# GpSimd's wide elementwise work is given to VectorE in a two-layer hybrid encoder, and the norm's steps are put in a new order

## The chip, the cores and the metric

The kernel runs on one core of one Trainium2 chip. The metric is the device time of one execution in microseconds (us), and a kernel's time is the median over its runs. TensorE (PE in the profile) multiplies matrices, VectorE (DVE) and ScalarE (ACT) do elementwise work and reductions, GpSimd (POOL) is a programmable engine that can do elementwise work too, and SyncE (SP) issues the transfers of the weights.

## The reference

256 tokens of width 1024 pass through two layers. Each layer has a SwiGLU FFN, a token mixing with three groups of heads, and a second FFN; every one of these six sub-layers is wrapped in an RMSNorm before and an RMSNorm after. Cut to what matters here:

```
for l in range(2):
    f = swiglu(rmsnorm(x, ffn1_pre_g[l]), ...);  x = x + 0.5 * rmsnorm(f, ffn1_post_g[l])
    m = token_mixing(rmsnorm(x, mix_pre_g[l]), ...);  x = x + rmsnorm(m, mix_post_g[l])
    f = swiglu(rmsnorm(x, ffn2_pre_g[l]), ...);  x = x + 0.5 * rmsnorm(f, ffn2_post_g[l])

# token mixing: one projection, three groups of heads, one output projection
A: softmax(q k^T / 8 + bias[head, clipped distance]) v            # 6 heads, bias is learned
B: (softmax(s0 + alibi) - lam * softmax(s1 + alibi)) v, normed      # 4 heads, alibi = -slope * distance
C: z = q k^T / 8;  a = exp(log_sigmoid(z) + suffix sum of log_sigmoid(-z)) v   # 6 heads, strictly causal
```

## The kernel before

All weights stream from memory in chunks of 512 KB. Each chunk is cut into a high and a low part: ScalarE rounds the chunk (L142, tile `whi`), VectorE subtracts the rounded part from the chunk (L143, tile `wlo`). TensorE then makes three products for each block of weights (L379 to L381, or L411 and L413 in the FFN), so that the sum is nearly float32. A class `Stream` hands the chunks out in a fixed order, up to nine chunks ahead of TensorE (more late in a sub-layer, where free tiles are lent to it), and each call of `ahead` issues half-chunk cuts on ScalarE and VectorE at the place in the program where it is called.

Everything runs in the order in which it is written: each engine takes its own instructions in program order and waits only for the semaphores of the tiles that it needs.

In the token mixing (`mix`), the projections of the queries and keys are 16 column blocks `pp` (L379 to L381), each in four quarters. After each quarter `slot(n)` runs the events whose time in the table PLAN lies below n + 1: the steps of the heads of B (`head_b`), of the pairs of heads of C (`pair_c`), of the heads of A (`head_a`), the moving of a finished block into `qkT` on ScalarE (`evacuate`, L845 and L847), and cuts of weight chunks. So the attention of one layer is interleaved with its own projections.

A pair of heads of C goes through these steps: the scores on TensorE (`s_c`, L670 and L671); the mask and a copy on VectorE (`z_c`, L674 and L676); three passes on ScalarE (L678 to L680) and one on VectorE (L682), which leave -log_sigmoid(-z) in `e`; the cut of `e` into high parts on ScalarE (`h1`, `h0`, L688 and L689) and low parts on GpSimd (`l1`, `l0`, L690 and L691); the suffix sums on TensorE (`u_c`, L694 to L701); the subtraction on VectorE (L703 and L704); the exponential on ScalarE (L706); the product with the values on TensorE (`o_c`, L745 and L746). For pair 0 these steps have the times 27.1 to 44.15 in PLAN: the suffix sums at 39.1, the subtraction at 39.15, the exponential at 39.2, the product at 42.05. The bias of A is negated in one instruction (`make_bias`, L643, 128 partitions by 1536 elements) at 41.05. `make_alibi` scales the distances for the four heads of B (L593, four instructions) before the first projection block.

At the end of a sub-layer, `down` accumulates the output of both halves of the tokens (t = 0 and 1), and `Norm` then does three things for each half: the norm of the output (L317, L291, L286), the residual sum into `xs` (L329, two halves of the width), and the norm that the next sub-layer needs (`half_pre`, `end_pre`): the mean square on ScalarE (L299, tile `junk_pre`), its sum on VectorE (L291, `v_pre`), the power -1/2 on GpSimd (L286, `r_pre`), the product of `xs` with the weights of the norm (L359, the first half of the width on GpSimd, the second on VectorE), and the scaling (L365 on VectorE, L366 on ScalarE). TensorE then turns the result (L374, tile `pt`). There are five such places between the six sub-layers, with two halves of the tokens each. For t = 0 the work of TensorE on the last chunks of t = 1 covers the norm; for t = 1 the first blocks of the next sub-layer do. The covering is shorter after a token mixing, which has four chunks for it where an FFN has five.

Of the kernel before, what the change touches and what calls it, by code (L numbers as in the profile page):

```python
# [9 lines left out]
F32 = mybir.dt.float32  # L10
# [3 lines left out]
ALU = mybir.AluOpType  # L14
# [150 lines left out]
def trunk_kernel(  # L165
# [7 lines left out]
    nc = tc.nc  # L173
# [123 lines left out]
    def mean_square(src, ss, h, nm):  # L297
        junk = work.tile([P, 512], BF16, tag="junk", name=f"junk_{nm}_{h}", bufs=1)
        nc.scalar.activation(junk, src, AF.Square, scale=ROOT, accum_out=ss[:, h : h + 1])  # L299
# [5 lines left out]
    class Norm:  # L305
# [6 lines left out]
        def post(self, banks, weight, slack=lambda k: None, last=None):  # L312
            i, t, nm = self.i - 1, self.t, "post" + self.nm
            ss = small.tile([P, 4], F32, tag="ss", name=f"ss_{nm}")
            fg = work.tile([P, D], F32, tag="fg", name=f"fg_{nm}", bufs=1)
            def gained(h):
                nc.vector.scalar_tensor_tensor(fg[:, HALVES[h]], banks[h], weight, post_tiles[i][:, HALVES[h]],  # L317
                                               ALU.mult, ALU.mult)

            for h in range(2):  # L320
                mean_square(banks[h], ss, h, nm)
            gained(0)
            r = rstd_of(halves_mean(ss, nm), 1, nm)
            gained(1)
            slack(0)
            if last is None:
                self.begin_pre()
            for h in range(2):
                nc.vector.scalar_tensor_tensor(xs[:, t, HALVES[h]], fg[:, HALVES[h]], r[:, 0:1],  # L329
                                               xs[:, t, HALVES[h]], ALU.mult, ALU.add)  # L330
                if last is None:
                    self.half_pre(h)
                else:
                    last(t, h)
            if last is None:
                self.end_pre()
                slack(1)
# [14 lines left out]
            self.ss = small.tile([P, 4], F32, tag="ss", name=f"sp_{self.nm}")  # L352
            self.xg = work.tile([P, D], F32, tag="xg", name=f"xg_{self.nm}", bufs=1)

        def half_pre(self, h):
            t, sl = self.t, HALVES[h]
            mean_square(xs[:, t, sl], self.ss, h, "pre" + self.nm)
            eng = nc.gpsimd if h == 0 else nc.vector
            eng.tensor_mul(self.xg[:, sl], xs[:, t, sl], pre_tiles[self.i][:, sl])  # L359

        def end_pre(self):
            self.r = rstd_of(halves_mean(self.ss, "pre" + self.nm), 1, "pre" + self.nm)

            xg = self.xg
            nc.vector.tensor_scalar(xg[:, :512], xg[:, :512], self.r[:, 0:1], None, ALU.mult)  # L365
            nc.scalar.activation(xg[:, 512:], xg[:, 512:], AF.Copy, scale=self.r[:, 0:1])  # L366

# [213 lines left out]
    def mix(i, l, turn1):  # L581
# [6 lines left out]
        def make_alibi():  # L588

            nc.vector.scalar_tensor_tensor(dneg, dist, -1.0, dist, ALU.mult, ALU.max)  # L590
            for h in range(NH_B):
                slope = 2.0 ** (-8.0 * (h + 1) / NH_B)
                nc.gpsimd.tensor_scalar(out=alibi[:, h, :], in0=dneg, scalar1=slope, scalar2=None, op0=ALU.mult)  # L593
            nc.gpsimd.memset(alibi[0:64, :, 192:256], FAR)

        def make_lambda():
# [43 lines left out]
        make_alibi()  # L640

        def make_bias():
            nc.gpsimd.tensor_scalar(out=biasA, in0=biasA, scalar1=-1.0, scalar2=None, op0=ALU.mult)  # L643
            nc.gpsimd.memset(biasA[0:64, :, 192:256], FAR)


# [2 lines left out]
        def pair_c(j):  # L649
# [37 lines left out]
            h1, l1 = hl1[:, :256], hl1[:, 256:]  # L687
            nc.scalar.copy(h1, e[:, 512:])  # L688
            nc.scalar.copy(h0, e[:, :512])  # L689
            nc.gpsimd.tensor_sub(l1, e[:, 512:], h1.bitcast(F32))  # L690
            nc.gpsimd.tensor_sub(l0, e[:, :512], h0.bitcast(F32))  # L691
            yield
            u1 = psum.tile([P, 256], F32, tag="acc", name=f"u1_{nm}")
            nc.tensor.matmul(u1, lhsT=tri, rhs=h1, start=True, stop=False)  # L694
# [276 lines left out]
```

## Time and profile before

| | |
|---|---|
| median of 3 runs | 1038.41 us (1036.89 to 1039.23) |
| profiled execution, its own time | 1042.82 us |
| span of the profile | 1041.1 us |
| TensorE busy | 1018.3 us, 98% of the span |
| VectorE busy | 676.4 us, 65% |
| ScalarE busy | 588.8 us, 57% |
| GpSimd busy | 89.0 us, 9% |
| mean granted TensorE clock | 0.986 of full speed |

The span runs from the first to the last instruction of one profiled execution, and all times inside the profile count from its start. Busy means that at least one instruction of the engine is in work. A granted clock of 1.00 is TensorE's level of 2.4 GHz, 0.50 is its level of 1.2 GHz.

### The profile page before, as it was taken

Reading aid. Unit: us, or ns where it says so; the run is one execution under the profiler, and the core shown is the slowest. Engines: PE = TensorE matmul, PEld = TensorE weight load, DVE = VectorE, ACT = ScalarE, POOL = GpSimd, SP = SyncE. Lnnn points to the kernel's source line nnn. Section 1 sums busy time; section 2 is a strip of 40 time slices with the busy share of each in tenths; the row PEclk is TensorE's granted clock in tenths of the full one; section 3 lists DMA queues with packets and bytes.
Section 4 is the critical chain, followed back from the end, with each engine's and each line's share of the span. In section 5 each row is a group of like instructions: output and inputs, shape, how many; then the busy total and the mean of one; then the engine's idle time right before and its main releaser. Section 6 shows DMA issues by size and latency. Waiting matters only on the chain. (4 is left out here: it accounts for less than half of the span.)

```text
span 1041.1 us, 16033 instructions
## 1 busy us (share of the span) xinstructions
PE 1018.3 (98%) x5940; PEld 888.6 (85%) x5940; DVE 676.4 (65%) x1313; ACT 588.8 (57%) x1265; POOL 89.0 (9%) x105
## 2 busy tenths in 40 slices
PE   8899999999999999999999999999999999999997
PEld 7788888898887988888899888888998789888886
DVE  4576774668666677665566876656776665877642
ACT  5465654567655556654446666545666655756531
POOL 3100000111311100000030000002123020000000
PEclk9999999999899999999999999999998999999999
DMA  8866566566244366656726766664933334865631
GB/s 270 219 204 200 184 211 208 145 203 192 82 122 122 117 210 220 197 189 219 215 73 208 244 195 195 222 198 121 261 107 103 117 97 143 261 190 186 222 120 40
DMA packets 151005, 183.16 MB, mean 176 GB/s; under 512 B 5744, under 2 KB 134896, under 8 KB 150928
## 3 DMA queue, kind: packets, MB, share of 16 engines
q1 hardware_dynamic: 148448, 174.08, 54.2%
q0 software_dynamic: 2192, 7.54, 2.7%
q8 instruction: 46, 0.75, 0.3%
q10 hardware_dynamic: 288, 0.52, 0.1%
q14 instruction: 31, 0.25, 0.1%
HBM read 181.08 MB, written 1.05 MB: 175 GB/s over the span
## 5 line engine op out<-in xcount | busy, mean ns | idle before, releaser
L143 DVE TENSOR_TENSOR wlo<-raw,whi 128x512 fp32r<-128x512 f32 (+1 forms) x625 | 403.2, 700 | 169.2 <-ACT whi L142 168.7
L142 ACT CAST whi<-raw 128x512 fp32r<-128x512 f32 x630 | 350.0, 617 | 120.5 <-PE acc L381 70.8
L411 PE MATMUL pg<-xT,whi 128*128 128x512 f32 x576 | 205.5, 398 | 0.0
L411 PE MATMUL pu<-xT,whi 128*128 128x512 f32 x576 | 203.2, 395 | 0.0
L413 PE MATMUL pg<-xT,wlo 128*128 128x256 f32 x576 | 162.2, 282 | 0.0
L413 PE MATMUL pu<-xT,wlo 128*128 128x256 f32 x576 | 161.5, 280 | 0.0
L379 PE MATMUL acc<-whi,hh 128*128 128x512 f32 x352 | 137.2, 390 | 0.0
L381 PE MATMUL acc<-whi,hl 128*128 128x512 f32 x352 | 137.0, 389 | 0.0
L380 PE MATMUL acc<-wlo,hh 128*128 128x512 f32 x352 | 137.0, 389 | 0.0
L411 PEld LDWEIGHTS pg<-xT,whi 128*128 128x128 f32 x576 | 108.7, 189 | 25.2
L411 PEld LDWEIGHTS pu<-xT,whi 128*128 128x128 f32 x576 | 108.0, 187 | 25.3
L413 PEld LDWEIGHTS pg<-xT,wlo 128*128 128x128 f32 x576 | 109.7, 190 | 0.0
L413 PEld LDWEIGHTS pu<-xT,wlo 128*128 128x128 f32 x576 | 108.8, 189 | 0.0
L379 PE MATMUL pp<-xT,whi 128*128 128x256 f32 x256 | 78.9, 308 | 0.0
L379 PEld LDWEIGHTS acc<-whi,hh 128*128 128x128 f32 x352 | 66.1, 188 | 13.7
L381 PEld LDWEIGHTS acc<-whi,hl 128*128 128x128 f32 x352 | 66.1, 188 | 13.7
L380 PEld LDWEIGHTS acc<-wlo,hh 128*128 128x128 f32 x352 | 66.1, 188 | 13.5
L380 PE MATMUL pp<-xT,whi 128*128 128x256 f32 x256 | 74.4, 291 | 0.0
L381 PE MATMUL pp<-xT,wlo 128*128 128x256 f32 x256 | 74.2, 290 | 0.0
L286 POOL TENSOR_TENSOR r_post<-v_post,mhalf 128x1 f32<-128x1 f32 x12 | 6.6, 552 | 779.5 <-DVE v_post L291 779.5
L379 PEld LDWEIGHTS pp<-xT,whi 128*128 128x128 f32 x256 | 51.0, 199 | 7.7 <-issue 7.2
L418 ACT COPY side_pu<-pu 128x256 f32<-128x256 f32 x72 | 26.1, 368 | 47.9 <-PE pu L413 47.9
(247 smaller groups left out, 1559.0 us busy)
## 6 DMA issues: line engine op xcount, KB each, us to landing
raw<-in_ffn_w_gate_dram SPq DMA_DIRECT2D x88, 512.0 KB, 4.8
raw<-in_ffn_w_up_dram SPq DMA_DIRECT2D x88, 512.0 KB, 4.7
raw<-in_ffn_w_down_dram SPq DMA_DIRECT2D x88, 512.0 KB, 4.4
raw<-in_w_in_dram SPq DMA_DIRECT2D x36, 512.0 KB, 5.6
raw<-in_w_out_dram SPq DMA_DIRECT2D x16, 512.0 KB, 3.5
raw<-in_w_in_dram SPq DMA_DIRECT2D x8, 576.0 KB, 4.5
gpost<-in_ffn_post_g_dram POOLq DMA_DIRECT2D x4, 512.0 KB, 4.6
raw<-in_w_in_dram SPq DMA_DIRECT2D x4, 384.0 KB, 3.5
```

Source lines behind the costliest of these rows:

```text
L142: self.nc.scalar.copy(self.hi[:, a:b], raw[:, a:b])
L143: (lo or self.nc.vector).tensor_sub(self.lo[:, a:b], raw[:, a:b], self.hi.bitcast(F32)[:, a:b])
L286: nc.gpsimd.tensor_tensor(r[:, :width], v, mhalf[:, :width], ALU.pow)
L379: nc.tensor.matmul(ps, lhsT=ah, rhs=bh, start=first, stop=False)
L380: nc.tensor.matmul(ps, lhsT=ah, rhs=bl, start=False, stop=False)
L381: nc.tensor.matmul(ps, lhsT=al, rhs=bh, start=False, stop=last)
L411: nc.tensor.matmul(ps.rearrange("p a t -> p (a t)"), lhsT=wh[:, k % 4, cs], rhs=xT[:, k].rearrange("p a t c -> p (a t c)"), start=k == 0, ...
L413: nc.tensor.matmul(ps[:, 1, :], lhsT=wl[:, k % 4, cs], rhs=xT[:, k, 0].rearrange("p t c -> p (t c)"), start=False, stop=k == KT - 1)
L418: nc.scalar.copy(side, ps[:, 1, :])
```

## The change

Four pieces of elementwise work go from GpSimd to VectorE: the negated bias of A, the four scalings of ALiBi, the low parts of `e` in group C (two instructions for each of the three pairs of a layer), and the first half of the product with the norm's weights. The two products of the norm, one for each half of the width, now stand on VectorE after both residual sums; the first stands ahead of the sum of the mean squares, the second behind it. The mean squares are issued where they were. GpSimd keeps the powers, the memsets, the iota, its transfers and the few cuts of weight chunks at the start.

```diff
@@ Norm.post
-                    self.half_pre(h)
+                    mean_square(xs[:, t, HALVES[h]], self.ss, h, "pre" + self.nm)
@@ Norm
-        def half_pre(self, h):
-            t, sl = self.t, HALVES[h]
-            mean_square(xs[:, t, sl], self.ss, h, "pre" + self.nm)
-            eng = nc.gpsimd if h == 0 else nc.vector
-            eng.tensor_mul(self.xg[:, sl], xs[:, t, sl], pre_tiles[self.i][:, sl])
-
         def end_pre(self):
-            self.r = rstd_of(halves_mean(self.ss, "pre" + self.nm), 1, "pre" + self.nm)
-
-            xg = self.xg
+            t, xg, g = self.t, self.xg, pre_tiles[self.i]
+
+            nc.vector.tensor_mul(xg[:, :512], xs[:, t, :512], g[:, :512])
+            v = halves_mean(self.ss, "pre" + self.nm)
+            nc.vector.tensor_mul(xg[:, 512:], xs[:, t, 512:], g[:, 512:])
+            self.r = rstd_of(v, 1, "pre" + self.nm)
             nc.vector.tensor_scalar(xg[:, :512], xg[:, :512], self.r[:, 0:1], None, ALU.mult)
             nc.scalar.activation(xg[:, 512:], xg[:, 512:], AF.Copy, scale=self.r[:, 0:1])
@@ make_alibi
-                nc.gpsimd.tensor_scalar(out=alibi[:, h, :], in0=dneg, scalar1=slope, scalar2=None, op0=ALU.mult)
+                nc.vector.tensor_scalar(out=alibi[:, h, :], in0=dneg, scalar1=slope, scalar2=None, op0=ALU.mult)
@@ make_bias
-            nc.gpsimd.tensor_scalar(out=biasA, in0=biasA, scalar1=-1.0, scalar2=None, op0=ALU.mult)
+            nc.vector.tensor_scalar(out=biasA, in0=biasA, scalar1=-1.0, scalar2=None, op0=ALU.mult)
@@ pair_c
-            nc.gpsimd.tensor_sub(l1, e[:, 512:], h1.bitcast(F32))
-            nc.gpsimd.tensor_sub(l0, e[:, :512], h0.bitcast(F32))
+            nc.vector.tensor_sub(l1, e[:, 512:], h1.bitcast(F32))
+            nc.vector.tensor_sub(l0, e[:, :512], h0.bitcast(F32))
```

The lines behind the edit in `Norm` move up by three, so L643 becomes L640, L690 becomes L687, L703 becomes L700 and so on. Three places on VectorE in the first layer's mixing; the second layer has the same three. The first is the stretch from the cuts behind the last pass of pair 0 to the subtraction of its sums (`yb` holds the `e` of pair 0, `wlo` are low parts of weights, `o_b` are outputs of B). Before:

```order
L143 TENSOR_TENSOR wlo_2804<-raw_2576,whi_2803 128x512 x2
L785 TENSOR_SCALAR yb_2378<-o_b_1_2834,rib_1_2563 128x64 x2
L785 TENSOR_SCALAR yb_2378<-o_b_0_2782,rib_0_2556 128x64 x2
L143 TENSOR_TENSOR wlo_2856<-raw_2611,whi_2855 128x512 x2
L703 TENSOR_TENSOR z_c_0_2741<-z_c_0_2741,u_c_0_2889 128x256
L704 TENSOR_TENSOR z_c_0_2741<-z_c_0_2741,u_c_0_2892 128x512
```

With the change:

```order
L143 TENSOR_TENSOR wlo_2804<-raw_2576,whi_2803 128x512
L687 TENSOR_TENSOR hl_c_0_2818<-yb_2378,hl_c_0_2818 128x256
L688 TENSOR_TENSOR l_c_0_2817<-yb_2378,h_c_0_2816 128x512
L143 TENSOR_TENSOR wlo_2804<-raw_2576,whi_2803 128x512
L782 TENSOR_SCALAR yb_2378<-o_b_1_2834,rib_1_2563 128x64 x2
L782 TENSOR_SCALAR yb_2378<-o_b_0_2782,rib_0_2556 128x64 x2
L143 TENSOR_TENSOR wlo_2856<-raw_2611,whi_2855 128x512 x2
L700 TENSOR_TENSOR z_c_0_2741<-z_c_0_2741,u_c_0_2889 128x256
L701 TENSOR_TENSOR z_c_0_2741<-z_c_0_2741,u_c_0_2892 128x512
```

The two low parts of pair 0 (`hl_c_0`, `l_c_0`) now stand on VectorE, between two cuts of weights and ahead of the subtraction.

The second place follows at once: the masks of pair 1, its pass L682 and the cut behind it. Before:

```order
L674 TENSOR_TENSOR z_c_1_2900<-s_c_1_0_2902,negmask 128x2x128
L676 COPY z_c_1_2900<-s_c_1_0_2902 128x128
L674 TENSOR_TENSOR z_c_1_2900<-s_c_1_1_2907,negmask 128x2x128
L676 COPY z_c_1_2900<-s_c_1_1_2907 128x128
L143 TENSOR_TENSOR wlo_2913<-raw_2670,whi_2912 128x512
L682 SCALAR_TENSOR_TENSOR e_c_1_2901<-z_c_1_2900,e_c_1_2901 128x768
L143 TENSOR_TENSOR wlo_2913<-raw_2670,whi_2912 128x512
```

With the change:

```order
L671 TENSOR_TENSOR z_c_1_2900<-s_c_1_0_2902,negmask 128x2x128
L673 COPY z_c_1_2900<-s_c_1_0_2902 128x128
L671 TENSOR_TENSOR z_c_1_2900<-s_c_1_1_2907,negmask 128x2x128
L673 COPY z_c_1_2900<-s_c_1_1_2907 128x128
L143 TENSOR_TENSOR wlo_2913<-raw_2670,whi_2912 128x512
L679 SCALAR_TENSOR_TENSOR e_c_1_2901<-z_c_1_2900,e_c_1_2901 128x768
L640 TENSOR_SCALAR yb_2378<-yb_2378 128x1536
L143 TENSOR_TENSOR wlo_2913<-raw_2670,whi_2912 128x512
```

The bias (128x1536, in another part of the tile `yb`) stands behind the subtraction of pair 0 and behind the last VectorE pass of pair 1. On GpSimd it stood right behind the low parts of pair 0.

The third place is further down, from the rounding of pair 0's output (`yC`) to the subtraction of pair 1's sums. Before:

```order
L303 TENSOR_TENSOR yC_2985<-o_c_0_2945,yC_2985 128x256
L143 TENSOR_TENSOR wlo_2969<-raw_2753,whi_2968 128x512
L682 SCALAR_TENSOR_TENSOR yb_2378<-z_c_2_2950,yb_2378 128x768
L143 TENSOR_TENSOR wlo_3023<-raw_2825,whi_3022 128x512 x2
L703 TENSOR_TENSOR z_c_1_2900<-z_c_1_2900,u_c_1_3050 128x256
L704 TENSOR_TENSOR z_c_1_2900<-z_c_1_2900,u_c_1_3053 128x512
```

With the change:

```order
L303 TENSOR_TENSOR yC_2985<-o_c_0_2945,yC_2985 128x256
L687 TENSOR_TENSOR hl_c_1_2990<-e_c_1_2901,hl_c_1_2990 128x256
L688 TENSOR_TENSOR l_c_1_2989<-e_c_1_2901,h_c_1_2988 128x512
L143 TENSOR_TENSOR wlo_2969<-raw_2753,whi_2968 128x512
L679 SCALAR_TENSOR_TENSOR yb_2378<-z_c_2_2950,yb_2378 128x768
L143 TENSOR_TENSOR wlo_3023<-raw_2825,whi_3022 128x512 x2
L687 TENSOR_TENSOR hl_c_2_3039<-yb_2378,hl_c_2_3039 128x256
L688 TENSOR_TENSOR l_c_2_3038<-yb_2378,h_c_2_3037 128x512
L700 TENSOR_TENSOR z_c_1_2900<-z_c_1_2900,u_c_1_3050 128x256
L701 TENSOR_TENSOR z_c_1_2900<-z_c_1_2900,u_c_1_3053 128x512
```

Pair 1's low parts stand ahead of a cut and of pair 2's pass, and pair 2's low parts, which wait for ScalarE's rounding of pair 2, now stand ahead of pair 1's subtraction.

## Rows read from the trace of the kernel before

**Rows 1.** The page: busy time, share of the span and instructions of each engine.

```profile
PE 1018.3 (98%) x5940; PEld 888.6 (85%) x5940; DVE 676.4 (65%) x1313; ACT 588.8 (57%) x1265; POOL 89.0 (9%) x105
```

**Rows 2.** Waits, whole span: us in total, times, longest us.

```profile
PE o_c L745 <- ACT yb L706: 4.2, 2, 2.1
PE pth L513 <- DVE ht L507: 3.9, 1, 3.9
...
PE pt L374 <- DVE xg L365: 1.4, 2, 0.7
...
PE s_b L750 <- ACT qkT L847: 0.6, 1, 0.6
...
PEld u_c L698 <- POOL l_c L691: 0.4, 2, 0.2
```

**Rows 3.** Stretches: us, busy PE, PEld, DVE, ACT, POOL, then granted clock, DMA.

```profile
273.30:275.40 2.10, 0.07 (x1) 0.00 (x0) 2.10 (x7) 0.82 (x2) 1.00 (x2) 1.00 0.34 66
275.70:285.90 10.20, 10.20 (x42) 8.55 (x39) 5.54 (x13) 8.10 (x14) 2.41 (x2) 0.50 0.21 82
278.40:285.10 6.70, 6.70 (x27) 6.07 (x27) 4.04 (x10) 5.47 (x11) 2.41 (x2) 0.50 0.22 82
784.30:794.50 10.20, 10.20 (x43) 9.25 (x42) 5.62 (x12) 7.13 (x12) 2.42 (x2) 0.50 0.25 71
43.60:46.90 3.30, 3.30 (x13) 2.81 (x12) 2.69 (x5) 1.14 (x3) 0.00 (x0) 0.50 0.80 218
```

**Rows 4.** Timeline of PE, first layer's mixing: start, us, what, idle before.

```profile
275.47 0.98 PE L745 MATMUL o_c<-yb,v 128*64 128x256 f32 x4 [2.10 <-ACT yb L706]
...
288.58 0.28 PE L694 MATMUL u_c<-hl_c,tri 128*128 128x256 f32 x1
...
294.55 0.66 PE L745 MATMUL o_c<-e_c,v 128*64 128x256 f32 x4
```

**Rows 5.** Timelines of DVE, POOL and ACT, same stretch.

```profile
267.54 0.69 DVE L143 TENSOR_TENSOR wlo<-raw,whi 128x512 fp32r<-128x512 f32 x1 [0.53 <-ACT whi L142]
...
268.92 4.64 DVE L143 TENSOR_TENSOR wlo<-raw,whi 128x512 fp32r<-128x512 f32 x2
273.48 0.41 DVE L703 TENSOR_TENSOR z_c<-z_c,u_c 128x256 f32<-128x256 f32 x1
...
269.36 4.53 POOL L643 TENSOR_SCALAR yb<-yb 128x1536 f32<-128x1536 f32 x1
...
274.58 0.84 ACT L706 ACTIVATE yb<-z_c 128x768 f32<-128x768 f32 x1 [5.07 <-DVE z_c L704]
```

**Rows 6.** VectorE's L143 from 268 to 274: ns min/median/max.

```profile
L143 DVE TENSOR_TENSOR wlo<-raw,whi x3: 693/1022/3696, 267.5 to 269.9; 128x512 fp32r<-128x512 f32 x3
```

**Rows 7.** Groups by form: busy us, mean ns of one, idle before.

```profile
L303 DVE TENSOR_TENSOR hl<-pth,hh 128x256 fp32r<-128x256 f32 x16 | 6.7, 419 | 3.5 <-ACT hh L302 3.5
...
L365 DVE TENSOR_SCALAR xg<-xg,r_pre 128x512 f32<-128x512 f32 x10 | 5.0, 500 | 7.0 <-POOL r_pre L286 7.0
...
L817 DVE TENSOR_SCALAR p_a<-p_a,ria 128x256 f32<-128x256 f32 x12 | 4.2, 348 | 0.0
```

**Rows 8.** Timelines of DVE, ACT and PE, norm behind the first layer's mixing.

```profile
335.26 1.67 DVE L359 TENSOR_TENSOR xg<-xs,gpre 128x512 f32<-128x512 f32 x1
336.86 0.20 DVE L291 TENSOR_SCALAR v_pre<-sp 128x1 f32<-128x1 f32 x1
...
335.95 0.19 ACT L299 ACTIVATION_READ_ACCUMULATOR junk_pre<-xs 128x1 f32 x1
...
338.25 1.10 PE L374 MATMUL pt<-ident,xg 128*128 128x128 f32 x8 [0.72 <-DVE xg L365]
```

**Rows 9.** Timeline of DVE at and behind ALiBi, first and second layer.

```profile
238.36 3.02 DVE L143 TENSOR_TENSOR wlo<-raw,whi 128x512 fp32r<-128x512 f32 x4
...
249.43 2.49 DVE L143 TENSOR_TENSOR wlo<-raw,whi 128x512 fp32r<-128x512 f32 x4
...
745.77 1.43 DVE L143 TENSOR_TENSOR wlo<-raw,whi 128x512 fp32r<-128x512 f32 x2 [0.21 <-ACT whi L142]
```

## The prediction

> **What bounds the kernel now.** I read the busy times first. TensorE is busy for 1018.3 us of the span of 1041.1 [rows 1]: its own work is the bound, and a change on two other engines can gain only where TensorE stands still or runs at its lower clock. GpSimd is busy for 89.0 us, VectorE for 676.4 [rows 1]; moving work between them matters only where TensorE waits for one of them.
>
> So the waits come next. TensorE waits twice for 2.1 us at the product of a pair of C (L745), for ScalarE's exponential L706; twice for 0.7 us at the turn of a norm (L374), for L365; once for 0.6 us at L750; the 3.9 us at L513 lie at the start, in lines that nobody touches [rows 2].
>
> Then the clock. In each layer, right behind the wait of 2.1 us, comes a stretch of 10.2 us with a granted clock of 0.50, the 1.2 GHz level; ahead of it the clock was 1.00 [rows 3]. The waits of 0.6 and 0.7 us are followed by no such stretch, the one of 3.9 us by a low stretch of 3.3 us [rows 2, 3]. A low stretch does in 10.2 us what takes 5.1 at the full clock. So each of the two places costs 2.1 + 5.1 = 7.2 us, and both together cost more than every other wait of the kernel.
>
> Last, why L706 is late. It waits for VectorE's subtraction (L703, L704), which stands behind two cuts of weights. VectorE needs 4.64 us for these two from 268.92 on; the same instruction takes 0.69 at its shortest, and the second of the two takes 3.70 [rows 5, 6]. Over that time GpSimd has the bias in work, from 269.36 for 4.53 us [rows 5]. Without GpSimd two cuts take 0.60 + 0.69 = 1.29: four take 2.49, so each starts 0.60 after the one before [rows 9]. The bias, off the path itself, thus makes VectorE 3.35 us late; ScalarE and TensorE pass that on.
>
> The Trainium skill has the mechanism (SBUF — State Buffer, Who interferes with whom): VectorE and GpSimd share one pair of ports as an exclusive lock, and a VectorE instruction with two inputs in SBUF is blocked for the whole of a GpSimd instruction that reads SBUF. The trace agrees in kind, with 3.70 against 0.69 us; taken literally the second cut would end after 273.89 + 0.60, but L703 starts at 273.48, so the sum goes by the row.
>
> **The change part by part, first layer.** *Pair 0.* VectorE gets the two low parts: 0.33 for 256 elements (0.419 alone [rows 7], less 0.09 overlap) and 0.60 for 512, together 0.93. They fall partly into the 0.53 us for which VectorE waits ahead of the cut at 267.54 [rows 5], so what follows starts about 0.4 later: the two cuts at 269.3 instead of 268.92, done at 270.5, the subtraction done 1.0 later (in the trace L706 starts 1.1 after L703 does, 273.48 to 274.58 [rows 5]), L706 from 271.6 to 272.4. TensorE stood ready for L745 at 275.47 - 2.10 = 273.4 [rows 4]. The wait of 2.1 goes, with 1.0 us to spare, because the bias now stands behind the subtraction in VectorE's order. With the wait I take the low clock to go too. Gain for both layers 2 x 2.1 = 4.2 and 2 x 5.1 = 10.2. TensorE's 0.2 us per layer for GpSimd's low parts (L698 [rows 2]) go as well: 0.4.
>
> *Bias.* One tensor-scalar instruction of 1536 elements on VectorE, which the trace has not. 256 elements take 0.348, 512 take 0.500 [rows 7], so 0.59 ns for each further element: 0.50 + 1024 x 0.59 ns = 1.1 us. The upper end takes the slope of two-input instructions, (0.693 - 0.419) / 256 = 1.07 ns [rows 6, 7]: 0.69 + 1.10 = 1.8. I take 1.1, since the nearest rows are the same operation on the same memory. At the far end stands GpSimd's own 4.53. It gains nothing by itself; it lies ahead of pair 1's low parts, and the question is whether these come late.
>
> *Pair 1, what is late next.* Everything behind L706 on ScalarE moves forward with it by 3.0 us, so pair 1's last VectorE pass starts at 275.4 instead of 278.4. From there to the place of the low parts VectorE has 4.04 us of work [rows 3]. With the bias (1.1) and the low parts (0.93) that is 6.1, so the low parts are done at 281.5. TensorE reaches pair 1's sums 288.58 - 275.47 = 13.1 us after L745 [rows 4]; at the full clock that is 8.0, so at 281.4, and needs the second low part some 0.3 later. This comes out even: a wait of 0 to 0.8 (the upper end with the bias at 1.8), I take 0.15 per layer.
>
> *Pair 1's exponential.* In the trace its L703 and L704 end 1.0 us after their place is reached, and L706 leaves TensorE's L745 at 294.55 about 3 us of slack. These 3 us are eaten: TensorE comes 5.97 us after the sums, at 287.4 [rows 4], while VectorE has behind 281.5 pair 2's pass (0.9), two cuts (1.2), pair 2's low parts (0.93) and the subtraction (1.0), with 0.84 for L706 behind them: 286.4, and a few tenths of waiting for ScalarE's passes of pair 2. Cost zero, by a margin of half a microsecond; without it the same tenths are lost there.
>
> *ALiBi.* Four scalings of 0.348 less 0.09 each: 1.05 us more on VectorE, ahead of the cuts at 238.36. Those four cuts took 3.02 instead of 2.49 because GpSimd scaled beside them [rows 9], so 0.5 us net. VectorE and ScalarE run in one chain from there to the block that TensorE waits for at L750 (0.6 us [rows 2]), so I count 0.5 in full. In the second layer VectorE has 0.21 us idle at that place, loses 0.14 (1.43 against 1.29 [rows 9]), and TensorE does not wait: 0 to 0.7, I take 0.2.
>
> *Norm.* VectorE's product L359 takes 1.67 us at 335.26 because GpSimd does the other half beside it; alone it takes 0.69 [rows 6, 8]. With the change the first product (0.60) hides the mean square, whose sum is there at 335.95 + 0.19 = 336.14 [rows 8]; the sum `v_pre` follows at 336.17 instead of 336.86, 0.69 earlier. The second product (0.69) lies under GpSimd's power, and the chain behind it is the same. TensorE waits 0.72 here [rows 8]; 0.67 of it goes. That happens twice: 1.3. At the other eight norms TensorE waits for no L365 [rows 2], so there the gain is nothing. If the low clock's cover had hidden anything there, it isn't seen: no low stretch touches them.
>
> Sum: 4.2 + 10.2 + 0.4 + 1.3 - 0.7 - 0.3 = 15.1 us. The profiled execution took 1042.82 for a span of 1041.1, so its own time would be 1027.7 and the span 1026.0. The median of the runs lies 4.4 us below that execution; 1038.41 - 15.1 = **1023.3**.
>
> **The rivals.** *The wait moves (same).* VectorE is without pause at the wait (2.10 of 2.10 us [rows 3]) and gets more work. If its chain to pair 1's sums is 2 us longer than my 6.1, TensorE waits there as long as it does now and loses the clock too: 7.2 per layer come back, and 0.4 + 1.3 - 0.7 = 1.0 is left: 1037.4. For it speaks that my margin there is nil; against it that the two bounds of the bias differ by only 0.7.
>
> The Trainium skill speaks for this one (Perfetto Trace Analysis, Optimizing Scalar/DVE Operations): a saturated VectorE is a reason to hand work to GpSimd, though it adds that between these two it might not help. No run here shows VectorE with this load.
>
> *VectorE becomes the bound (slower).* If it is more than 2 us late at pair 1's sums and again, by pair 2's low parts, at pair 1's L745, there are two waits of 2.1 with a low stretch each: 14.4 per layer instead of 7.2, so 1038.4 + 14.4 - 1.0 = 1051.8. It needs a chain a third longer than reckoned, twice. *The clock stays low.* If the low stretch has another cause than the wait, only 4.2 + 1.0 - 0.3 = 4.9 is gained: 1033.5. Against it: it follows the wait in both layers, with the same 10.2 us [rows 3]. *A short low stretch at ALiBi.* The wait at L750 grows from 0.6 to 1.1 in the first layer, between 0.7, after which the clock never fell, and 2.1, after which it fell both times. A low stretch of 3.3 to 10.2 us costs 1.7 to 5.1: 1025.0 to 1028.4.
>
> **How the numbers follow.** As forecast 0.62, a low stretch at ALiBi 0.12, clock stays low 0.07, the wait moves 0.12 (half of it in part, as a loss of some 7 us), slower 0.07. The likeliest alone runs from 1020 (no cost at ALiBi and at pair 1, 1.0 together, and two microseconds for the runs) to 1026 (the bias at 1.8 with tenths lost at both places). To leave out no more than 2 in 10 the range takes in the low clock at ALiBi and the clock that stays low, with a microsecond for the runs: 1019 to 1034. About 0.2%, 2 us, is what a measurement of this kernel can tell from no change. Faster 0.86, same 0.07, slower 0.07.
>
> **What would show it.** Right: no wait at pair 0's L745 (now L742), a granted clock of 1.00 from 264 to 330, VectorE's cuts at 0.69 throughout, the bias near 1.1 us, GpSimd busy for half of its 89 us or less, VectorE within some 10 us of its 676, `v_pre` 0.7 earlier in each norm, TensorE's L750 wait near 1.1. Wrong: a wait above a microsecond at pair 1's sums or product; a stretch at 0.50 behind 47 us; a bias instruction of 3 us or more.

## The result, and the profile after

The changed kernel takes 1030.78 us (median of 7 runs, 1027.78 to 1032.34) against 1039.29 for the kernel before in the same series (7 runs, 1036.89 to 1047.22): a ratio of 0.9901, interval 0.9874 to 0.9927. It is faster, and inside the range of the prediction, but the gain is some 10 us and not 15: the medians lie 8.5 us apart, the means 11.3 (1041.59 and 1030.26). Its profiled execution took 1030.83, where 1027.7 was forecast, with a span of 1029.1.

The page of the changed kernel, busy times:

```profile
PE 1011.4 (98%) x5940; PEld 881.9 (86%) x5940; DVE 673.2 (65%) x1345; ACT 588.1 (57%) x1265; POOL 43.2 (4%) x73
```

GpSimd lost half of its 89 us, and VectorE, which took all of it over, is no busier than before [rows 1]. Per mixing it got 0.90 us of ALiBi, 0.95 of bias and three times 0.93 of low parts, and 0.60 in each of ten norms: 15.3 in all. The groups by form pay it back: the cuts (613 of L143) fall from 395.4 to 388.1 us, and the ten products that it had before (L359, now L360) from 1.67 to 0.68 each.

TensorE's waits in the changed kernel, which answer to [rows 2] (us in total, times, longest):

```profile
PE pth L510 <- DVE ht L504: 3.1, 1, 3.1
...
PE pt L371 <- DVE xg L362: 1.0, 2, 0.5
...
PE s_b L747 <- ACT qkT L844: 0.4, 1, 0.4
```

The product of pair 0 (now L742) is gone from the list, and so are the sums of C. The turn of the norm still waits, 0.5 instead of 0.7 us.

Stretches ahead of and behind pair 0's product in both layers, columns as in [rows 3]:

```profile
264.00:275.00 11.00, 11.00 (x91) 10.56 (x90) 7.92 (x22) 8.38 (x16) 0.00 (x0) 1.00 0.40 124
275.00:285.20 10.20, 10.20 (x76) 9.02 (x74) 8.40 (x18) 9.45 (x18) 0.41 (x1) 1.00 0.26 81
764.00:775.50 11.50, 11.50 (x97) 11.13 (x96) 8.82 (x23) 7.85 (x16) 0.00 (x0) 1.00 0.37 105
775.50:785.70 10.20, 10.20 (x77) 9.05 (x76) 8.00 (x17) 9.46 (x17) 0.41 (x1) 1.00 0.28 90
```

The granted clock is 1.00 behind the product: 76 matmuls in 10.2 us, where 42 ran before.

VectorE from pair 0's low parts to the subtraction of pair 1's sums, then TensorE's products and sums, first layer:

```profile
268.84 0.42 DVE L687 TENSOR_TENSOR hl_c<-yb,hl_c 128x256 fp32r<-128x256 f32 x1
269.17 0.69 DVE L688 TENSOR_TENSOR l_c<-yb,h_c 128x512 fp32r<-128x512 f32 x1
...
271.14 1.29 DVE L143 TENSOR_TENSOR wlo<-raw,whi 128x512 fp32r<-128x512 f32 x2
272.34 0.42 DVE L700 TENSOR_TENSOR z_c<-z_c,u_c 128x256 f32<-128x256 f32 x1
...
278.21 0.95 DVE L640 TENSOR_SCALAR yb<-yb 128x1536 f32<-128x1536 f32 x1
...
282.39 0.69 DVE L688 TENSOR_TENSOR l_c<-e_c,h_c 128x512 fp32r<-128x512 f32 x1
...
286.93 0.69 DVE L701 TENSOR_TENSOR z_c<-z_c,u_c 128x512 f32<-128x512 f32 x1
```

```profile
275.07 0.66 PE L742 MATMUL o_c<-yb,v 128*64 128x256 f32 x4
...
283.56 0.28 PE L691 MATMUL u_c<-hl_c,tri 128*128 128x256 f32 x1
...
289.54 0.66 PE L742 MATMUL o_c<-e_c,v 128*64 128x256 f32 x4
```

The two cuts take 1.29 us instead of 4.64 [rows 5]. The bias takes 0.95 on VectorE. Pair 1's low parts end at 283.08, half a microsecond ahead of its sums, and nothing is late there.

The norm behind the first layer's mixing, on VectorE, GpSimd and TensorE, which answers to [rows 8]:

```profile
330.19 0.68 DVE L358 TENSOR_TENSOR xg<-xs,gpre 128x512 f32<-128x512 f32 x1
331.22 0.21 DVE L291 TENSOR_SCALAR v_pre<-sp 128x1 f32<-128x1 f32 x1 [0.34 <-ACT junk_pre L299]
331.35 0.68 DVE L360 TENSOR_TENSOR xg<-xs,gpre 128x512 f32<-128x512 f32 x1
...
331.57 0.86 POOL L286 TENSOR_TENSOR r_pre<-v_pre,mhalf 128x1 f32<-128x1 f32 x1 [2.75 <-DVE v_pre L291]
...
333.02 1.09 PE L371 MATMUL pt<-ident,xg 128*128 128x128 f32 x8 [0.50 <-DVE xg L362]
```

The sum `v_pre` follows the mean square at once, as forecast, but the power takes 0.86 us while VectorE's second product runs beside it. The power of the output's norm, the same instruction without that neighbour, takes 0.55 in the same trace (median of 12).

**Where the 12.0 us between the two profiles lie.** The first row of TensorE's turns (L374, L371) marks the end of each sub-layer:

| from turn to turn | before | changed | difference |
|---|---|---|---|
| start and first FFN | 203.39 | 205.85 | +2.46 |
| first mixing | 134.86 | 127.17 | -7.69 |
| second FFN | 187.62 | 187.31 | -0.31 |
| third FFN | 185.74 | 187.25 | +1.51 |
| second mixing | 134.20 | 126.50 | -7.70 |
| fourth FFN, end | 195.29 | 195.02 | -0.27 |

The mixings give back 15.4 us. The first and third FFN lose, in lines that the change does not touch. Stretches of 85 us inside the gate and up products, the first, second and third FFN of the kernel before, then the third of the changed one:

```profile
55.00:140.00 85.00, 85.00 (x492) 74.95 (x491) 62.14 (x113) 52.26 (x110) 0.00 (x0) 1.00 0.64 200
375.00:460.00 85.00, 85.00 (x483) 73.67 (x482) 62.73 (x113) 53.39 (x113) 0.00 (x0) 1.00 0.68 211
560.00:645.00 85.00, 85.00 (x492) 74.91 (x492) 63.51 (x114) 55.14 (x116) 0.00 (x0) 1.00 0.68 210
```

```profile
560.00:645.00 85.00, 85.00 (x483) 73.78 (x482) 62.21 (x112) 53.58 (x112) 0.00 (x0) 1.00 0.67 209
```

With the same granted clock of 1.00 and no wait, TensorE does 492 matmuls or 483. The whole stretch of an FFN is some 1.8 us longer at the slower pace (187.25 - 185.74, and the 0.3 that the norm gained). The first execution of the kernel before had the faster pace in two of its FFNs, that of the changed kernel in none.

### The profile page after: what moved, and what is told of

Its sections match the earlier page's. It is cut to its first block, busy times and chain, and to the rows that moved or that the text cites. A ratio compares the mean times of both kernels' runs of the same rounds, so it can differ in the third digit from the quotient of the medians.

```text
span 1029.1 us, 16023 instructions
## 1 busy us (share of the span) xinstructions
PE 1011.4 (98%) x5940; PEld 881.9 (86%) x5940; DVE 673.2 (65%) x1345; ACT 588.1 (57%) x1265; POOL 43.2 (4%) x73
## 4 chain that ended last, share of the span: by engine, by line
PE 89%; DMA 3%; ACT 3%; DVE 3%; POOL 1%; issue 1%; SPq 0%; POOLq 0%; DVEq 0%; ACTq 0%
PE pg L408 13%; PE pu L408 13%; PE acc L376 9%; PE acc L378 9%; PE acc L377 9%; PE pg L410 7%; PE pu L410 7%; PE pp L376 3%; PE pp L377 2%; PE pp L378 2%; DMA raw<-in_ffn_w_gate_dram 2%; DVE wlo L143 1%; PE pu L377 1%; PE pu L378 1%; PE pu L376 1%; PE pg L376 1%
## 5 line engine op out<-in xcount | busy, mean ns | idle before, releaser
L143 DVE TENSOR_TENSOR wlo<-raw,whi 128x512 fp32r<-128x512 f32 (+1 forms) x625 | 395.9, 689 | 159.3 <-ACT whi L142 158.8
L377 PE MATMUL acc<-wlo,hh 128*128 128x512 f32 x352 | 137.0, 389 | 0.0
L377 PEld LDWEIGHTS acc<-wlo,hh 128*128 128x128 f32 x352 | 66.1, 188 | 13.5
L376 PE MATMUL pp<-xT,whi 128*128 128x256 f32 x256 | 76.2, 298 | 0.0
L377 PE MATMUL pp<-xT,whi 128*128 128x256 f32 x256 | 72.3, 282 | 0.0
L376 PEld LDWEIGHTS pp<-xT,whi 128*128 128x128 f32 x256 | 48.8, 191 | 7.3 <-issue 6.3
L416 DVE TENSOR_TENSOR h<-pu,side_pu 128x256 f32<-128x256 f32 x72 | 29.8, 422 | 29.6 <-ACT side_pu L415 29.4
```

Of the source, the lines that this page charges most:

```text
L143: (lo or self.nc.vector).tensor_sub(self.lo[:, a:b], raw[:, a:b], self.hi.bitcast(F32)[:, a:b])
L376: nc.tensor.matmul(ps, lhsT=ah, rhs=bh, start=first, stop=False)
L377: nc.tensor.matmul(ps, lhsT=ah, rhs=bl, start=False, stop=False)
L416: nc.vector.tensor_add(out[:, j, :], ps[:, 0, :], side)
```

## The experiments

My theory: one GpSimd instruction, the bias, makes VectorE late, TensorE waits, and the low clock follows the wait. The rivals: GpSimd's low parts have a share; the order of the work did the harm, not GpSimd's access to memory; the low clock has another cause than the wait. Open besides: why some 10 us and not 15.

All series, with the mean granted clock over the runs (it is listed with every run). A ratio stands for one series against the kernel before in the same series; for the kernel before it is that of its 12 runs to its 23, for the changed kernel that of its second series:

| kernel | median us (runs) | ratio to before, interval | mean clock |
|---|---|---|---|
| before, twice in one series (23 and 12 runs) | 1040.9 (35) | 1.0004 [0.9974, 1.0033] | 0.988 |
| changed, first series and again | 1030.7 (13) | 0.9896 [0.9866, 0.9926] | 0.9935 |
| bias only, on VectorE | 1032.67 (6) | 0.9913 [0.9885, 0.9941] | 0.993 |
| bias only, on ScalarE | 1032.22 (5) | 0.9912 [0.9883, 0.9941] | 0.994 |
| bias in three, on GpSimd | 1029.63 (6) | 0.9894 [0.9864, 0.9925] | 0.994 |
| changed, bias on GpSimd | 1037.59 (12) | 0.9967 [0.9946, 0.9989] | 0.990 |
| changed, idle 16-bit work on GpSimd | 1029.21 (4) | 0.9884 [0.9854, 0.9913] | 0.9935 |
| changed, late exponential | 1041.78 (12) | 1.0003 [0.9985, 1.0021] | 0.986 |
| changed, ScalarE and products first | 1030.56 (5) | 0.9915 [0.9876, 0.9954] | 0.993 |

Three kernels ran once each, for their traces: both products first (1029.38 us), the bias held back (1033.62) and the idle work in two other forms (1031.09).

**The kernel before, again.** No edit. Expected:

> The kernel before, unchanged. First theory on the shortfall (chance of the execution): of the four FFN stretches some run their 512-column products at a median of 391 ns and some at 398, another number of them than the two and two of the first profile, and the start differs by a microsecond; both mixings hold the wait of 2.1 us at L745 and 10 us at a clock of 0.50. Second theory (a property of the kernel): again the first and the third FFN at 391, the second and fourth at 398. Third (the low stretch is not in every execution): one of the two mixings without its low stretch, and a span some 5 us shorter, 1036. Ratio to the kernel before 1.00 within its interval.

TensorE at pair 0's product in both layers, and the stretches behind:

```profile
274.82 0.66 PE L745 MATMUL o_c<-yb,v 128*64 128x256 f32 x4 [2.08 <-ACT yb L706]
...
779.81 0.66 PE L745 MATMUL o_c<-yb,v 128*64 128x256 f32 x4 [2.09 <-ACT yb L706]
```

```profile
275.30:285.50 10.20, 10.20 (x74) 8.98 (x71) 7.85 (x16) 9.88 (x18) 3.08 (x3) 1.00 0.34 117
780.00:790.20 10.20, 10.20 (x75) 8.86 (x72) 7.55 (x15) 10.07 (x19) 2.79 (x3) 1.00 0.34 125
```

Both waits are there, at 2.1 us, and the clock stays at 1.00 behind both. The span is 1033.3 instead of 1041.1. So the wait belongs to the kernel, the low stretch only to some of its executions; that is the third expectation, for both layers at once. The mixings take 130.61 and 129.86 us here: a low stretch costs 134.86 - 130.61 = 4.25 and 134.20 - 129.86 = 4.34, not the 5.1 that I reckoned. The rows say why: in the low stretch of the first profile, products of 256 columns start 0.21 to 0.22 us apart, behind it 0.12, so the half clock slows them by 1.8 and not by 2.

```profile
279.19 0.41 PE L379 MATMUL pp<-xT,whi 128*128 128x256 f32 x1
279.41 0.41 PE L380 MATMUL pp<-xT,whi 128*128 128x256 f32 x1
...
286.07 0.28 PE L379 MATMUL pp<-xT,whi 128*128 128x256 f32 x1
286.19 0.28 PE L380 MATMUL pp<-xT,whi 128*128 128x256 f32 x1
```

The first FFN runs at the faster pace, the third at the slower (187.54), so the pace too changes from one execution to the next.

**The changed kernel, again.** Expected:

> The changed kernel, unchanged. Chance of the execution: some FFN at 391 ns, the span between 1024 and 1030, the stretch from the first to the second mixing's end as in the first profile of it (127.2 and 126.5 us for the two mixings). Property of the change: all four FFN at 398 again and a span of 1029. Ratio 0.988 to 0.991; 0.986 if the median of the forecast was right.

Span 1029.0, mixings 127.77 and 126.48, the first FFN at the faster pace. The ratio of 0.9896 repeats the first.

**The bias alone on VectorE**, the rest as before.

```diff
-            nc.gpsimd.tensor_scalar(out=biasA, in0=biasA, scalar1=-1.0, scalar2=None, op0=ALU.mult)
+            nc.vector.tensor_scalar(out=biasA, in0=biasA, scalar1=-1.0, scalar2=None, op0=ALU.mult)
```

> The kernel before with the bias alone on VectorE. If the bias holds VectorE's second cut, and that is the cause of the wait: no wait at pair 0's L745, VectorE's cuts at 0.69 there, no stretch at 0.50 in either mixing, each mixing 7.0 to 7.3 us shorter than before, and nearly all of the change's gain: ratio 0.988 to 0.992, within 1.5 us of the whole change. If the low parts on GpSimd have a share in it: a wait of 0.5 to 1.5 us stays at L745, and the ratio is 0.993 or higher.

```profile
271.15 1.62 DVE L143 TENSOR_TENSOR wlo<-raw,whi 128x512 fp32r<-128x512 f32 x2
...
275.55 0.66 PE L745 MATMUL o_c<-yb,v 128*64 128x256 f32 x4
```

No wait at L745, clock 1.00, mixings of 127.73 and 127.61, ratio 0.9913. With GpSimd's low parts still ahead of the two cuts these take 1.62 us, not 1.29; that is all their share. The bias is most of the change: the rest of it is worth 0.6 and 1.1 us of the two mixings and 0.3 us in each of three FFN stretches, and the median lies 2.2 us above that of the whole change in the same series (1032.67 and 1030.46), where I expected 1.5 at most.

**The changed kernel with the bias back on GpSimd.**

```diff
-            nc.vector.tensor_scalar(out=biasA, in0=biasA, scalar1=-1.0, scalar2=None, op0=ALU.mult)
+            nc.gpsimd.tensor_scalar(out=biasA, in0=biasA, scalar1=-1.0, scalar2=None, op0=ALU.mult)
```

> The changed kernel with the bias alone given back to GpSimd. GpSimd has nothing ahead of it then and starts it behind ALiBi, some 28 us earlier than before, near 241.5. If a GpSimd instruction holds VectorE wherever it lies: a VectorE instruction with two inputs from memory near 242 to 246 takes about 3 us longer, the softmax chain of B is late, and TensorE waits 2 to 3.5 us at L747, with a stretch at 0.50 behind it; pair 0's L742 has no wait; ratio 0.995 to 1.00. If the harm came from the order of the work alone (the bias between the low parts and the sums): no wait of over 0.8 us anywhere in the mixing and the time of the changed kernel, ratio 0.988 to 0.991.

VectorE, GpSimd and TensorE in the first layer:

```profile
239.92 5.51 DVE L143 TENSOR_TENSOR wlo<-raw,whi 128x512 fp32r<-128x512 f32 x4
...
240.34 4.21 POOL L640 TENSOR_SCALAR yb<-yb 128x1536 f32<-128x1536 f32 x1
...
253.17 0.50 PE L747 MATMUL s_b<-qkT 32*128 32x128 f32 x4 [3.41 <-ACT qkT L844]
```

GpSimd runs the bias 29 us earlier (240.34, against 269.36 in [rows 5]), four cuts take 5.51 instead of 2.49, one of them 3.7, and TensorE waits 3.41 at another product (3.17 in the second layer). The harm moved with the instruction: it is no matter of the place in the order. In this execution a low stretch of only 3.3 us follows (254.8 to 258.1, clock 0.51), in the second layer one of 3.4; the mixings take 130.53 and 130.29 us.

**Idle work on GpSimd, 16-bit output**, behind pair 0's low parts in the changed kernel.

```diff
             nc.vector.tensor_sub(l0, e[:, :512], h0.bitcast(F32))
+            if j == 0:
+                for n in range(3):
+                    idle = work.tile([P, 512], BF16, tag="junk", name=f"idle_{nm}_{n}", bufs=1)
+                    nc.gpsimd.tensor_scalar(out=idle, in0=l0.bitcast(F32), scalar1=-1.0, scalar2=None, op0=ALU.mult)
```

> The changed kernel with three added GpSimd instructions (512 elements each, from pair 0's low part into a scratch tile that nobody reads), which can start when VectorE has written the low part, near 269.8. Nothing waits for them. If a GpSimd instruction holds VectorE's two-input instructions: VectorE's cuts and the subtraction behind 269.8 take 2 to 4 us longer in sum, the margin of 0.8 us is used up, TensorE waits 1 to 3 us at pair 0's L742, and the time goes half of the way back or more, ratio 0.993 to 1.00. If the order or the data was the cause and not the shared memory access: VectorE's cuts at 0.69, no wait at pair 0, ratio 0.988 to 0.991.

```profile
269.43 1.28 DVE L143 TENSOR_TENSOR wlo<-raw,whi 128x512 fp32r<-128x512 f32 x2
...
268.24 5.40 POOL L692 TENSOR_SCALAR idle_c<-l_c 128x512 bf16<-128x512 f32 x3 [28.49 <-DVE l_c L688]
```

My expectation fails: GpSimd works for 5.40 us across both cuts, and they take 1.28 in sum. "GpSimd holds VectorE" is too wide. It could be the type, the length, or the rewriting in place; the next two runs separate them.

**The bias held back on GpSimd**, in the changed kernel, in one piece in the first layer and in three in the second.

```diff
-            nc.vector.tensor_scalar(out=biasA, in0=biasA, scalar1=-1.0, scalar2=None, op0=ALU.mult)
+            pin = work.tile([P, 256], F32, tag="junk", name=f"pin{l}", bufs=1)
+            nc.gpsimd.tensor_copy(pin[:, :8], low[0][:, :8].bitcast(F32))
+            if l == 0:
+                nc.gpsimd.tensor_scalar(out=biasA, in0=biasA, scalar1=-1.0, scalar2=None, op0=ALU.mult)
+            else:
+                for n in range(3):
+                    part = yb[:, 512 + 512 * n : 1024 + 512 * n]
+                    nc.gpsimd.tensor_scalar(out=part, in0=part, scalar1=-1.0, scalar2=None, op0=ALU.mult)
...
+            low[j] = l0
```

> The changed kernel with the bias on GpSimd, held back there by a copy of eight columns until VectorE has written pair 0's low part, so that it stands where it stood before. First layer: one instruction of 1536 elements, as before; second layer: three of 512. If the 32-bit bias holds VectorE whatever its length: in both layers VectorE's two cuts ahead of pair 0's subtraction take 2 to 4 us instead of 1.29, and TensorE waits 0.7 to 2.5 us at L742. If only the long instruction does: the first layer so, the second with cuts of 1.29 to 1.6 and no wait. If GpSimd alone is not enough and it took GpSimd's low parts too: 1.29 in both.

VectorE's two cuts, GpSimd's bias and TensorE's product, first layer, then the two in the second:

```profile
267.68 3.72 DVE L143 TENSOR_TENSOR wlo<-raw,whi 128x512 fp32r<-128x512 f32 x2
...
267.02 4.10 POOL L645 TENSOR_SCALAR yb<-yb 128x1536 f32<-128x1536 f32 x1
...
273.31 0.66 PE L752 MATMUL o_c<-yb,v 128*64 128x256 f32 x4 [1.62 <-ACT yb L713]
...
775.08 1.28 DVE L143 TENSOR_TENSOR wlo<-raw,whi 128x512 fp32r<-128x512 f32 x2
...
774.42 4.75 POOL L649 TENSOR_SCALAR yb<-yb 128x512 f32<-128x512 f32 x3
```

Same data, same types, same place, same work: in one piece one cut takes 3.1 us, in three pieces none is touched. It is the length of the one instruction. The wait of 1.62 is followed by 10.2 us at the low clock (0.53 from 273.8 to 284.0), and the mixing takes 133.20; the second layer has 126.58.

**Idle work in two other forms**: in the changed kernel, six instructions of 256 elements with 32-bit output behind pair 0's low parts, tensor-scalar in the first layer, two-input in the second.

> The changed kernel with six added GpSimd instructions of 256 elements with 32-bit output, read by nobody, from pair 0's low part on: tensor-scalar in the first layer, two-input subtractions in the second. The three instructions with 16-bit output of the run before did not hold VectorE. If the 32-bit output makes the difference: VectorE's cuts ahead of the subtraction take at least 0.5 us more in the first layer. If also two-input instructions hold it: in the second layer too, 1.5 us or more. If it is the in-place rewriting or the length of the bias: 1.29 in both layers.

GpSimd works for 7.22 and 6.67 us, the cuts take 1.28 in both layers, mixings of 127.27 and 126.79. A single cut further down, beside the two-input form, takes 1.18 instead of 0.69. So short instructions cost VectorE nothing or tenths.

**The bias in three pieces, in the kernel before.** Nothing is moved.

```diff
-            nc.gpsimd.tensor_scalar(out=biasA, in0=biasA, scalar1=-1.0, scalar2=None, op0=ALU.mult)
+            for n in range(3):
+                part = yb[:, 512 + 512 * n : 1024 + 512 * n]
+                nc.gpsimd.tensor_scalar(out=part, in0=part, scalar1=-1.0, scalar2=None, op0=ALU.mult)
```

> The kernel before with nothing moved: the bias stays on GpSimd at its place and is done in three instructions of 512 elements instead of one of 1536. If it is the length of the one instruction that holds VectorE, as the run with the bias held back shows: VectorE's two cuts take 1.3 to 1.9 us, no wait at pair 0's L745, no stretch at 0.50 in the mixings, each of them 127.4 to 128.2 us long, and the ratio of the bias alone on VectorE, 0.988 to 0.994. If GpSimd's work at this place is harmful in any form once its low parts stand ahead of it: cuts of 3 us or more, the wait of 2 us as before, ratio 0.998 to 1.002.

```profile
270.61 2.03 DVE L143 TENSOR_TENSOR wlo<-raw,whi 128x512 fp32r<-128x512 f32 x2
...
271.05 4.84 POOL L645 TENSOR_SCALAR yb<-yb 128x512 f32<-128x512 f32 x3
...
275.00 0.66 PE L747 MATMUL o_c<-yb,v 128*64 128x256 f32 x4
```

GpSimd works 0.3 us longer than with the one instruction, and the wait is gone: the cuts take 2.03 (1.02 and 1.09, a little over the 1.9 that I set as the upper end), TensorE's product does not wait in either layer, and the clock stays at 1.00 in the mixings. They take 127.94 and 127.34 us, and the ratio is 0.9894. This one edit, with all of the work left on GpSimd, gains as much as the whole change as far as the runs can tell (some 3 us either way). By its stages it gives what moving the bias alone gave: 255.28 us for both mixings, against 255.34 there and 253.7 to 254.3 in the changed kernel.

**The bias alone on ScalarE**, in the kernel before.

```diff
-            nc.gpsimd.tensor_scalar(out=biasA, in0=biasA, scalar1=-1.0, scalar2=None, op0=ALU.mult)
+            nc.scalar.mul(biasA, biasA, -1.0)
```

> The kernel before with the bias alone on ScalarE. If what matters is that the bias leaves GpSimd, and not that VectorE does it: no wait at pair 0's L745, VectorE's cuts at 0.69 there, the mixings within 0.5 us of those with the bias alone on VectorE (127.7 and 127.6), ratio 0.988 to 0.993. The instruction takes about 1.5 us on ScalarE by the slope from 512 to 768 elements. If it makes ScalarE late for pair 1's roundings instead: a wait of up to 1.5 us at pair 1's sums (L694).

1.47 us on ScalarE, no wait at L745 or L694, mixings 127.35 and 127.76: it does not matter which engine takes it from GpSimd.

**A late exponential**: ScalarE alone is made late, in the changed kernel, by four copies that the exponential overwrites.

```diff
+            if j == 0:
+                for n in range(4):
+                    nc.scalar.activation(e, z, AF.Copy)
             nc.scalar.activation(e, z, AF.Exp)
```

> The changed kernel with four added ScalarE copies ahead of pair 0's exponential (their result is overwritten): ScalarE alone is made about 3.5 us late, GpSimd and VectorE do no more than in the changed kernel. TensorE's margin there is 0.8 us, so it should wait 2.5 to 2.9 us at pair 0's L742 in each layer. If a wait of any origin at this place can bring the low clock: some executions show a stretch at 0.50 behind it, the mean granted clock over the runs falls from 0.9935 (changed kernel) toward 0.988 (kernel before), and the mean time is 5 to 12 us above the changed kernel's. If the low clock belonged to GpSimd's work and not to the wait: mean clock 0.9935 as in the changed kernel, and only the two waits are added, 5 to 6 us.

TensorE's product in the first layer (L745 here, moved down three lines by the edit), then the stretches behind it in both:

```profile
276.39 1.13 PE L745 MATMUL o_c<-yb,v 128*64 128x256 f32 x4 [2.70 <-ACT yb L706]
```

```profile
276.60:286.80 10.20, 10.20 (x44) 8.46 (x43) 6.21 (x14) 8.12 (x14) 0.41 (x1) 0.53 0.19 54
784.90:795.10 10.20, 10.20 (x43) 8.46 (x42) 6.22 (x14) 8.11 (x14) 0.41 (x1) 0.52 0.17 53
```

A wait of 2.7 us without any work on GpSimd brings the low stretch in both layers, and over 12 runs the mean clock falls from 0.9935 to 0.986. The mean time rises by 12.0 us (1030.19 to 1042.17), of which the two waits are 5.4. So a wait brings the low clock without any work on GpSimd, though not in every execution, as the second profile of the kernel before shows.

**Both products ahead of the sum**, in the changed kernel's norm.

```diff
-            v = halves_mean(self.ss, "pre" + self.nm)
             nc.vector.tensor_mul(xg[:, 512:], xs[:, t, 512:], g[:, 512:])
+            v = halves_mean(self.ss, "pre" + self.nm)
```

> The changed kernel with both products of the norm ahead of the sum of the mean squares. In the changed kernel the power on GpSimd takes 0.86 us where VectorE's second product runs beside it, and 0.55 elsewhere. If VectorE's product holds GpSimd's power: the power takes 0.55, the sum comes 0.3 later than in the changed kernel, L362 starts within 0.15 of where it did, and the wait at the turn is 0.35 to 0.55 us instead of 0.50. If the power was slow for another reason: it takes 0.86 still, and the wait grows to 0.7 to 0.8.

The power takes 0.55, the waits at the turn 0.7 us in sum instead of 1.0. So VectorE's product does hold GpSimd's power; a tenth or two per norm is what the order can win back.

**ScalarE for the bias and both products first**, in the changed kernel.

> The changed kernel with the bias on ScalarE and both products of the norm ahead of the sum, the best parts so far. If VectorE's added load costs anything in the changed kernel: mixings 0.3 to 1 us shorter than 127.2 and 126.5, ratio 0.986 to 0.989. If the load lies beside TensorE's work, as I think: the mixings within 0.4 us, and a ratio of 0.987 to 0.992, not to be told from the changed kernel's.

Mixings of 127.06 and 127.05, 254.1 in sum against 253.7 and 254.3 of the two profiles of the changed kernel. VectorE's load costs nothing there, and no version measured here beats the changed kernel by more than a measurement can tell.

## Why the prediction was right, and where it was not

**Pair 0: right.** Wait gone, cuts at 1.29, TensorE's margin 0.8 us where I said 1.0. By the profiles the mixings gave 7.69 and 7.70; my terms that fall there made 7.4 and 7.7 (with the norm's 0.67 each). That this agrees so well is partly luck: the low stretch was worth 4.3 and not 5.1 and the norm's wait 0.2 and not 0.67, while ALiBi and pair 1 cost nothing and each mixing gained 0.4 us at its start that I had not counted.

**The low clock: right in cause, wrong in size, and this is the step that failed.** "With the wait I take the low clock to go too" holds: late exponentials bring it, and none of the nine profiles without a wait of over 1.5 us in the mixings shows it there. But the 10.2 us of the sum took it as a fixed part of the kernel before, from one execution that had it in both layers. The second profile of that kernel has it in neither. Over the 35 runs of the kernel before a mean clock of 0.988 leaves 0.0120 x 1040.9 = 12.5 us of full clock not granted, over the 13 of the changed kernel 0.0065 x 1030.2 = 6.7. The difference of 5.8 stands against the 10.2 of the sum: about one low stretch in an execution rather than two. In time it is less, since two stretches cost 4.25 + 4.34 = 8.6 us: 5.8 x 8.6 / 10.2 = 4.9, an estimate. The other terms I summed to 15.1 - 10.2 = 4.9; by the rows they gave some 6.5 (the two waits 4.2, the suffix sums 0.2, the norm 2.1, no cost for ALiBi and pair 1). That makes 11.4, where the means differ by 10.75 (1040.94 to 1030.19); the runs cannot tell the two apart.

**The base: the same error a second time.** I worked the sum out on an execution of 1042.82 and took it off a median of 1038.41. The 4.4 us between the two are a sign that the profiled execution held something that others lack, and I named them without asking what. Part of them was the chance of three runs: the median of 35 is 1040.9.

**The range held by luck.** For the forecast alone I gave 1020 to 1026, and 1030.78 lies outside. The stated range reaches to 1034 because I had widened it for a clock that stays low and for a low stretch at ALiBi; neither came.

**Between the two profiles** the forecast was 15.1 and 12.0 came. The mixings and the norms gave more than that together (15.4 and 0.9); two FFNs at the slower pace took 3.6 back and the start some 0.7. Both are differences between executions: the faster pace turned up in either kernel, and not always in the same FFNs.

**Norm: 2.1 in sum instead of 1.3, most of it in other places.** The two waits lost 0.2 each and not 0.67, mostly since the second product, which I laid under GpSimd's power without a price, makes the power 0.3 longer. In return 0.3 us went in each of three FFN stretches where I had counted nothing: TensorE's eight transposes for t = 1 take 1.03 us instead of 1.33 there; the wait lay inside the row and was not in the list of waits. Behind the first layer's mixing, before and changed:

```profile
347.78 1.33 PE L374 MATMUL pt<-ident,xg 128*128 128x128 f32 x8
```

```profile
342.53 1.03 PE L371 MATMUL pt<-ident,xg 128*128 128x128 f32 x8
```

At the start of each mixing 0.4 us went too: from the turn for t = 1 to the next chunk's second product (`pv`, L380, now L377) TensorE took 2.47 us (212.94 to 215.41) and takes 2.10 (215.42 to 217.52).

**ALiBi: no cost instead of 0.7.** From the negated distances (L590, now L587) to the first softmax of B (L726, L723) VectorE takes 6.22 us where it took 6.15. Four scalings came in, and the cuts and the small steps of lambda that GpSimd had slowed beside them became as much shorter. The rival of a low stretch at ALiBi is out: L747 waits 0.4, and none follows.

**Pair 1: right, with a margin of half a microsecond** where I had it even. The bias took 0.95, below my lower bound of 1.1. So the rivals of a wait that moves and of VectorE as the bound did not come; the saturated VectorE on which the advice of the Trainium skill rests (Perfetto Trace Analysis, Optimizing Scalar/DVE Operations) is not this one, at 65% busy.

**The mechanism is narrower than I had it.** A cut beside the one long instruction took 3.1 to 3.7 us in four profiles (the kernel before twice, the bias back on GpSimd, the bias held back), beside instructions of up to 512 elements 0.68 to 1.2, with GpSimd busy as long in sum. Two products started side by side (the norm before, 512 elements each) lie between, 1.67 for 0.69 [rows 8]. The Trainium skill (SBUF — State Buffer, Who interferes with whom) makes their shared ports an exclusive lock, so that a VectorE instruction with two inputs in SBUF would stand still for the whole of a GpSimd one that reads there; the three idle instructions of 512, 5.40 us in sum beside two cuts of 1.28, do not agree. Why length decides, and why two products of 512 elements side by side still cost 1.0 us, stays open.

## What to carry to other kernels

Look for single long instructions on GpSimd beside a chain on VectorE that TensorE waits for, and first try to cut the instruction into pieces: here that gained as much as moving four pieces of work, as far as the runs can tell. Before a low-clock stretch goes into a sum, see in several executions how often it occurs, and take the sum off an execution of the same kind. Here a wait of two microseconds on TensorE cost its own length in every execution and about four more in some.

## What the runs showed of the hardware that was not expected

The same wait of 2.1 us was followed by 10 us at half clock in one execution of a kernel and by none in another; a wait of 1.62 by 10 us, one of 3.41 by only 3.3. TensorE's gate and up products run at one of two paces, 492 or 483 matmuls in 85 us at a granted clock of 1.00, for a whole FFN at a time, in either kernel; what decides was not tried. VectorE can hold GpSimd as well: a power of one element per partition takes 0.86 instead of 0.55 us beside VectorE's product. And the executions of the kernel before spread over 15 us (1032.68 to 1048.14), those of the changed kernel over 6 (1026.78 to 1032.34).
